# A two-layer hybrid block: x also loaded by columns, first-layer S5 angles on GpSimd, wider kpe and gate products

## The chip, the cores and the metric

The kernel runs on one core of a Trainium2 chip. Its time is that of one execution on the device in microseconds (us); three executions of the kernel before gave 883.68, 882.55 and 882.38, median 882.55. The engines are TensorE (PE in the profile: matrix products and transposes; PEld is its weight load), VectorE (DVE), ScalarE (ACT), GpSimd (POOL) and SyncE (SP), whose queue issues nearly all transfers. Each engine runs its own instructions in a fixed order and waits on semaphores of the others.

## The reference

256 tokens of width 1024 (f32) pass two layers. In each, a normed h is projected once, and three mixers share the columns: latent attention (MLA, 8 heads), a gated linear attention in chunks of 64 (GLA, 4 heads) and a diagonal state-space scan (S5, 32 groups of 64 complex states).

```
h = rms_norm(x, norm1_g[l])
(cq, ckv, kpe, gq, gk, gv, glr, gr, su, gates) = split_in(h @ w_in[l])
o_a = mla_mixer(cq, ckv, kpe, ...)
o_b = gla_mixer(gq, gk, gv, glr, gr, ...)     # log_a = log_sigmoid(g_lr @ w_gate + b_gate) / 16
o_c = s5_mixer(su, ...)                       # lam_bar = exp(lam * step); states by associative scan
g = sigmoid(gates + gate_b[l]).reshape(B, L, 3, D)
merged = g[:,:,0]*(o_a @ w_br_mla[l]) + g[:,:,1]*(o_b @ w_br_gla[l]) + g[:,:,2]*(o_c @ w_br_s5[l])
x = x + merged @ w_out[l]
h2 = rms_norm(x, norm2_g[l])
x = x + square(relu(h2 @ w_ff1[l])) @ w_ff2[l]
```

The kernel does the S5 scan in a rotating frame: it needs, for each of 16 x 128 states, the sine and cosine of angle times position. These depend on the parameters alone.

## The kernel before, in words

**Tiling.** h is kept by columns: 8 tiles of 128 features by 256 tokens, each as a rounded part (hi) and a rest (lo). The weights lie in HBM as 276 chunks of 128x1024 f32 (512 KB). `fetch` (L139) loads a chunk into one of three buffers raw, the first two chunks in halves; `prep` (L155) splits it: ScalarE casts hi (L164), VectorE subtracts to lo (L165). Every product is three: hi by hi, hi by lo, lo by hi (L184 to L186). Chunks are prepared three ahead, in four buffers.

**Start.** `setup` (L264) loads x by token rows in four pieces, with the constants between them, on SyncE's queue. `norm` (L508) turns x by 16 transposes on TensorE (L520), VectorE multiplies by the gain (xs, L523), ScalarE and VectorE split to h. The norm's factor is not put into h: `norm_end` (L529) squares x on ScalarE, VectorE makes the reciprocal root (nr) and two scaled unit matrices dg (L549), and in `norm_rows` TensorE makes from them a row of factors for all partitions, rb (L555), with which later results are multiplied.

**Order of the work.** `mixers` (L1232) walks a hand-written table, STEPS (L1171), one string for each layer. An entry names a step and the offset of its priority: "kg~53" is the next piece of the step kg, 53 further back. The scheduler then places each engine's instructions by priority. qk, kg, gate, gv, gr, core, gout are GLA; ckv, cq, kv, v, kT, q, qT, h, p are attention; su, u, v0 to s3 and y are S5; g and b entries are the gates and the branch products. "P" is the next piece of `s5_pre` (L334), which makes the S5 constants of the first layer between the other steps. The second layer's constants are made during the first layer's feed-forward.

**S5 constants.** `s5_pre` makes roots and exponentials on 128x16 tiles with VectorE, then bbar and cmat (ScalarE spreads z, L418), which TensorE transposes (Btp, L453) and multiplies (K0p, L462). The angles follow (L471 to L499): for each of four tiles ph of 128x512, VectorE multiplies the position iota by the high part of the angle thi, takes off the whole turns (kk, in the buffer cosT), adds iota times the low part (four operations, L485) and takes off the whole turns again. ScalarE makes sine, half-angle sine and its square (L493 to L495), VectorE the cosine from the square (L499). GpSimd does only memsets and the copies R (L606).

**GLA around the change.** `gla_qk` (L903): 96 products of 256 columns to gqkp, rb, then gqk = gqkp times rb. `kpe_glr` (L682): a product kgp of 128 rows, of which rows 0 to 31 are the rotary key and 32 to 47 the gate's low-rank input; kgT = kgp times rb on 48 rows, two transposes of 32 rows (L690). `gla_gate` (L932): four products of 16 rows, gatep (L937), then log sigmoid, a scan cs, its exponentials ep and en, and with them the scores Ap (L977) and the state terms dS.

Of the kernel before, what the change touches and what calls it, by code (L numbers as in the profile page):

```python
# [8 lines left out]
F32 = mybir.dt.float32  # L9
F32R = mybir.dt.float32r  # L10
# [8 lines left out]
DEPTH = 2  # L19
D = 1024  # L20
# [66 lines left out]
class Kern:  # L87
# [51 lines left out]
    def fetch(self, k):  # L139
        l, c = self.stream[k]  # L140
        n = CCOLS.get(c[0], CW)
        raw = self.ring.tile([128, CW], F32, tag="raw", name="raw", bufs=self.NRAW)
        for h in self.halves(k, n):
            self.nc.sync.dma_start(raw[:, h], self.wst[l, CIDX[c], :, h])
        self.raws.append(raw)

    def halves(self, k, n):

        return [slice(0, n // 2), slice(n // 2, n)] if k < self.NHALF else [slice(0, n)]

# [4 lines left out]
    def prep(self, k):  # L155
# [7 lines left out]
        for h in self.halves(k, n):  # L163
            nc.scalar.copy(hi[:, h], raw[:, h])  # L164
            nc.vector.tensor_tensor(out=lo[:, h], in0=raw[:, h], in1=hi[:, h].bitcast(F32), op=ALU.subtract)  # L165
# [86 lines left out]
    def split(self, hi, lo, src, scale=None):  # L252

        nc = self.nc
        if scale is None:
            nc.scalar.copy(hi, src)  # L256
# [7 lines left out]
    def setup(self):  # L264
# [5 lines left out]
        xl = lambda t, n: load(self.x[:, t, n * 512:(n + 1) * 512], self.xin[t * 128:(t + 1) * 128, n * 512:(n + 1) * 512])  # L270
        o = KOFF["iota"][0]
        xl(0, 0)
        load(con[:, 0:o], self.consts[:, 0:o])
        xl(1, 0)
        self.prefetch(1)
        xl(0, 1)
        xl(1, 1)
        self.prefetch(3)
        self.load_par(0)
        load(con[:, o:], self.consts[:, o:KOFF["caus"][0]])  # L280
# [9 lines left out]
        self.sin = k("sin").rearrange("p (t d) -> p t d", t=NT)  # L290

# [42 lines left out]
    def s5_pre(self, l):  # L334
# [135 lines left out]

        phs = [self.s2(f"Q{4 + i}", "ph") for i in range(4)]  # L471
        sinT, cosT = self.b8(1, "sinT"), self.b8(0, "cosT")
        kk = cosT
        for i in range(4):
# [15 lines left out]
        for i in range(4):  # L490
            c = slice(512 * i, 512 * i + 512)
            ph = phs[i]
            nc.scalar.activation(sinT[:, c], ph, AF.Sin, scale=TURN)  # L493
            nc.scalar.activation(ph, ph, AF.Sin, scale=TURN / 2)
            nc.scalar.activation(cosT[:, c], ph, AF.Square)  # L495
# [11 lines left out]
    def norm(self, l, key, n):  # L507
# [17 lines left out]
        if l or key == "n2g":  # L525
            self.norm_end(l, key, n)
# [155 lines left out]
    def kpe_glr(self, l):  # L682
# [4 lines left out]
        nc.vector.tensor_tensor(out=self.kgT[0:48], in0=p[0:48], in1=self.rb[0:48], op=ALU.mult)  # L687
        p = self.pt("kpe", [128, NT, 32])
        for t in range(NT):
            nc.tensor.transpose(p[:, t, :], self.kgT[0:32, t * 128:(t + 1) * 128], self.ident[0:32, 0:32])  # L690
        self.kpe = self.tiny.tile([128, NT, 32], F32, tag="kpe", name="kpe", bufs=1)
        nc.scalar.copy(self.kpe, p)
# [239 lines left out]
    def gla_gate(self, l):  # L932
# [3 lines left out]
        for m in range(2):  # L936
            nc.tensor.matmul(p[:, m, :], lhsT=wg[32:48, m * 128:(m + 1) * 128], rhs=self.kgT[32:48], start=True, stop=True)  # L937
# [211 lines left out]
    def ff2_end(self, l, n, po):  # L1149
# [13 lines left out]
    NHALF = 2  # L1163
# [79 lines left out]
    def run(self):  # L1243
# [138 lines left out]
```

## Time and profile before

| | |
|---|---|
| median of three executions | 882.55 us |
| the profiled execution, its span | 882.19 us, 880.4 us |
| TensorE busy | 861.7 us, 98% |
| VectorE busy | 694.5 us, 79% |
| ScalarE busy | 522.0 us, 59% |
| GpSimd busy | 25.4 us, 3% |
| mean granted TensorE clock | 0.998 |
| read from HBM, over the span | 145.70 MB, 167 GB/s |

The span runs from the first to the last instruction. The first layer's mixers end at about 239 us, when the product wo begins; its feed-forward fills the time to 452; the second layer's mixers run from there to 675, its feed-forward to the end. A row of the timeline gives start and duration; matmuls are pipelined, so the distance from one start to the next, not the duration, is what one costs. In rows of a stretch the count of instructions stands in brackets, and PEclk is the granted share of TensorE's full clock (1.00 is 2.4 GHz).

### The profile page before, as it was taken

Reading aid. Unit: us, or ns where it says so; the run is one execution under the profiler, and the core shown is the slowest. Engines: PE = TensorE matmul, PEld = TensorE weight load, DVE = VectorE, ACT = ScalarE, POOL = GpSimd, SP = SyncE. Lnnn points to the kernel's source line nnn. Section 1 sums busy time; section 2 is a strip of 40 time slices with the busy share of each in tenths; the row PEclk is TensorE's granted clock in tenths of the full one; section 3 lists DMA queues with packets and bytes.
Section 4 is the critical chain, followed back from the end, with each engine's and each line's share of the span. In section 5 each row is a group of like instructions: output and inputs, shape, how many; then the busy total and the mean of one; then the engine's idle time right before and its main releaser. Section 6 shows DMA issues by size and latency. Waiting matters only on the chain.

```text
span 880.4 us, 15290 instructions
## 1 busy us (share of the span) xinstructions
PE 861.7 (98%) x5900; PEld 771.2 (88%) x5900; DVE 694.5 (79%) x1339; ACT 522.0 (59%) x818; POOL 25.4 (3%) x35
## 2 busy tenths in 40 slices
PE   7999999999999999999999999999999999999998
PEld 6889988899988888888888989898999888888886
DVE  7999999987767986996677887899877776666664
ACT  6877887654456575664457647874554654444442
POOL 2000001010000000000000000002000000000000
PEclk9999999999999999999999999999999999999999
DMA  7534434245564565566545544244555555555562
GB/s 265 188 118 143 154 121 145 72 153 177 189 210 153 186 212 168 182 189 203 190 146 168 191 146 150 97 144 135 178 166 170 191 181 192 189 189 188 192 190 92
DMA packets 42264, 147.73 MB, mean 168 GB/s; under 512 B 4688, under 2 KB 5328, under 8 KB 42192
## 3 DMA queue, kind: packets, MB, share of 16 engines
q1 hardware_dynamic: 42192, 146.76, 51.6%
q8 instruction: 46, 0.75, 0.3%
q14 instruction: 26, 0.21, 0.1%
HBM read 145.70 MB, written 1.05 MB: 167 GB/s over the span
## 4 chain that ended last, share of the span: by engine, by line
PE 84%; DVE 10%; ACT 3%; issue 2%; DMA 1%; SPq 0%; DVEq 0%
PE fp L206 14%; PE fp L210 7%; PE fo L184 7%; PE fo L186 7%; PE fo L185 7%; PE gp L184 3%; DVE lo L165 3%; PE gp L185 3%; PE gp L186 3%; PE brp L184 2%; PE brp L186 2%; PE brp L185 2%; PE wo L186 2%; PE wo L184 2%; PE wo L185 2%
## 5 line engine op out<-in xcount | busy, mean ns | idle before, releaser
L165 DVE TENSOR_TENSOR lo<-raw,hi 128x1024 fp32r<-128x1024 f32 (+2 forms) x276 | 333.0, 1208 | 118.6 <-ACT hi L164 117.5
L164 ACT CAST hi<-raw 128x1024 fp32r<-128x1024 f32 (+2 forms) x276 | 286.1, 1038 | 234.0 <-PE fo L186 52.9
L206 PE MATMUL fp<-h,hi 128*128 128x512 f32 x512 | 180.5, 398 | 0.0
L210 PE MATMUL fp<-h,lo 128*128 128x256 f32 x512 | 133.5, 281 | 0.0
L184 PE MATMUL gp<-h,hi 128*128 128x256 f32 x384 | 109.9, 292 | 1.0 <-ACT ppt L875 0.8
L206 PEld LDWEIGHTS fp<-h,hi 128*128 128x128 f32 x512 | 93.9, 188 | 18.1
L186 PE MATMUL gp<-h,lo 128*128 128x256 f32 x384 | 107.8, 286 | 0.0
L185 PE MATMUL gp<-h,hi 128*128 128x256 f32 x384 | 107.4, 285 | 0.0
L210 PEld LDWEIGHTS fp<-h,lo 128*128 128x128 f32 x512 | 96.8, 189 | 5.5
L184 PE MATMUL fo<-hi,r 128*128 128x512 f32 x256 | 100.1, 391 | 0.0
L186 PE MATMUL fo<-hi,r 128*128 128x512 f32 x256 | 99.7, 390 | 0.0
L185 PE MATMUL fo<-lo,r 128*128 128x512 f32 x256 | 99.7, 389 | 0.0
L184 PEld LDWEIGHTS gp<-h,hi 128*128 128x128 f32 x384 | 72.7, 192 | 2.9 <-ACT ppt L875 1.0
L185 PEld LDWEIGHTS gp<-h,hi 128*128 128x128 f32 x384 | 72.6, 191 | 1.0 <-issue 0.5
L186 PEld LDWEIGHTS gp<-h,lo 128*128 128x128 f32 x384 | 72.7, 192 | 0.1
L185 PEld LDWEIGHTS fo<-lo,r 128*128 128x128 f32 x256 | 48.1, 188 | 10.1
L186 PEld LDWEIGHTS fo<-hi,r 128*128 128x128 f32 x256 | 48.1, 188 | 10.2
L184 PEld LDWEIGHTS fo<-hi,r 128*128 128x128 f32 x256 | 48.1, 188 | 8.8
L1133 ACT COPY fa<-fp 128x256 f32<-128x256 f32 x64 | 23.4, 367 | 29.3 <-PE fp L206 29.1
L1134 DVE TENSOR_TENSOR fa<-fa,fp 128x256 f32<-128x256 f32 x64 | 26.2, 416 | 13.7 <-ACT fa L1133 13.7
L1071 ACT ACTIVATE gt<-gt,hgateb 128x256 f32<-128x256 f32 x48 | 21.9, 501 | 9.0 <-DVE gt L1068 8.8
L256 ACT CAST r<-fa 128x512 fp32r<-128x512 f32 x32 | 19.9, 622 | 9.7 <-DVE fa L1135 9.5
(396 smaller groups left out, 1768.0 us busy)
## 6 DMA issues: line engine op xcount, KB each, us to landing
raw<-wst SPq DMA_DIRECT2D x266, 512.0 KB, 3.6
raw<-wst SPq DMA_DIRECT2D x6, 384.0 KB, 3.0
x<-xin SPq DMA_DIRECT2D x4, 256.0 KB, 4.6
raw<-wst SPq DMA_DIRECT2D x4, 256.0 KB, 5.6
bc_raw<-bcin SPq DMA_DIRECT2D x4, 256.0 KB, 3.8
out_dram<-x SPq DMA_DIRECT2D x4, 256.0 KB, 2.0
par<-parin SPq DMA_DIRECT2D x2, 205.0 KB, 5.8
masks<-consts SPq DMA_DIRECT2D x1, 128.0 KB, 3.8
```

The source lines that it names most:

```text
L164: nc.scalar.copy(hi[:, h], raw[:, h])
L165: nc.vector.tensor_tensor(out=lo[:, h], in0=raw[:, h], in1=hi[:, h].bitcast(F32), op=ALU.subtract)
L184: mm(out, lhsT=lt[0], rhs=rt[0], start=start, stop=False)
L185: mm(out, lhsT=lt[0], rhs=rt[1], start=False, stop=False)
L186: mm(out, lhsT=lt[1], rhs=rt[0], start=False, stop=stop)
L206: up = lambda: mm(flat, lhsT=w[0][:, c], rhs=self.h2[:, k].rearrange("p i t -> p (i t)"), start=k == 0, stop=k == KD - 1)
L210: mm(out[:, 0, :], lhsT=w[1][:, c], rhs=self.h[k][0], start=False, stop=False)
L256: nc.scalar.copy(hi, src)
L1071: nc.scalar.activation(g[:, m, :], g[:, m, :], AF.Tanh, scale=0.5, bias=self.small[l]["gateb"][:, c:c + 1])
L1133: nc.scalar.copy(a[:, m], p[:, 1, :])
L1134: self.mark = v.tensor_tensor(out=a[:, m], in0=a[:, m], in1=p[:, 0, :], op=ALU.add)
```

## The change

1. x is passed a second time by columns (`xtin`), loaded into xT by four transfers on ScalarE's queue. `begin_x` splits h straight from it, with the gain as the scale. `norm` isn't called for the first h; `norm_end` is, for the norm's factor, from token rows of x that are now loaded after the first six chunks.
2. The first chunks are loaded and split in pieces, chunk 0 as two quarters and a half, chunks 1 to 3 in halves, in the order of the string BEGIN, into four of the large buffers.
3. The first layer's angles are made by GpSimd. The four operations of L485 become two on the whole tile. ScalarE's sines are kept behind a certain cast in its order.
4. kgT, the kpe transposes and the gate products use all 128 rows.
5. The step qk has two pieces: products, then rb and what it multiplies. Both tables STEPS are new.

```diff
-            nc.scalar.copy(hi, src)
+            self.cast = nc.scalar.copy(hi, src)
             nc.vector.tensor_tensor(out=lo, in0=src, in1=hi.bitcast(F32), op=ALU.subtract)
...
         self.ident = k("ident")
         self.ng = k("ng")
+        i0 = KOFF["ng"][0]
+        load(con[:, i0:o], self.consts[:, i0:o])
+
+        self.begin()
+        for a in self.BEGIN.split():
+            n, i = a[0], int(a[1:])
+            if n == "x":
+                self.begin_x(i)
+            elif n in "wh":
+
+                m = 4 if n == "w" else 2
+                self.begin_w(i // m, (i % m) * CW // m, CW // m)
+            elif n == "t":
+                load(self.x[:, i, :], self.xin[i * 128:(i + 1) * 128, :])
+            elif n == "f":
+                self.prefetch(i)
+            elif n == "p":
+                self.load_par(0)
+                load(con[:, 0:i0], self.consts[:, 0:i0])
+                load(con[:, o:], self.consts[:, o:KOFF["caus"][0]])
...
+    def begin(self):
+        self.new_h()
+        self.nss = self.tiny.tile([128, 2, NT], F32, tag="nss", name="nss", bufs=2)
+        self.xT = self.b8(6, "xT").rearrange("p (k t) -> p k t", k=KD)
+        hl = lambda n: self.ring.tile([128, CW], F32R, tag=n, name=n, bufs=self.NHI)
+
+        self.raws = [self.b8(i, "raw", cols=2048)[:, 0:CW] for i in (0, 1, 4, 8)]
+
+        for k in range(0, KD, 2):
+            self.nc.scalar.dma_start(self.xT[:, k:k + 2, :], self.xtin[:, k * L:(k + 2) * L])
+        for k in range(4):
+            self.prepped[k] = (hl("hi"), hl("lo"))
+
+    def begin_x(self, k):
+
+        nc = self.nc
+        self.split(self.h[k][0], self.h[k][1], self.xT[:, k, :], scale=self.ng[:, k:k + 1])
+
+    def begin_w(self, k, o, n):
+        l, c = self.stream[k]
+        h = slice(o, o + n)
+        self.nc.sync.dma_start(self.raws[k][:, h], self.wst[l, CIDX[c], :, h])
+        self.split(*(y[:, h] for y in self.prepped[k]), self.raws[k][:, h])
...
+        if l == 0:
+            v, tt = nc.gpsimd, nc.gpsimd.tensor_tensor
         phs = [self.s2(f"Q{4 + i}", "ph") for i in range(4)]
...
-            for j in range(4):
-                v.scalar_tensor_tensor(out=ph3[:, j], in0=self.iota, scalar=tlo[:, 4 * i + j:4 * i + j + 1],
-                                       in1=ph3[:, j], op0=ALU.mult, op1=ALU.add)
+            if l:
+                for j in range(4):
+                    v.scalar_tensor_tensor(out=ph3[:, j], in0=self.iota, scalar=tlo[:, 4 * i + j:4 * i + j + 1],
+                                           in1=ph3[:, j], op0=ALU.mult, op1=ALU.add)
+            else:
+                tt(out=kk[:, c].rearrange("p (s c) -> p s c", s=4), in0=self.iota.unsqueeze(1).to_broadcast(b3),
+                   in1=tlo[:, 4 * i:4 * i + 4].unsqueeze(2).to_broadcast(b3), op=ALU.mult)
+                tt(out=ph, in0=ph, in1=kk[:, c], op=ALU.add)
...
+        with self.tc.issue_after(self.cast.ins):
+            for i in range(4):
...
-        nc.vector.tensor_tensor(out=self.kgT[0:48], in0=p[0:48], in1=self.rb[0:48], op=ALU.mult)
-        p = self.pt("kpe", [128, NT, 32])
+        nc.vector.tensor_tensor(out=self.kgT, in0=p, in1=self.rb, op=ALU.mult)
+        p = self.pt("kpe", [128, NT, 128])
         for t in range(NT):
-            nc.tensor.transpose(p[:, t, :], self.kgT[0:32, t * 128:(t + 1) * 128], self.ident[0:32, 0:32])
+            nc.tensor.transpose(p[:, t, :], self.kgT[:, t * 128:(t + 1) * 128], self.ident)
...
-            nc.tensor.matmul(p[:, m, :], lhsT=wg[32:48, m * 128:(m + 1) * 128], rhs=self.kgT[32:48], start=True, stop=True)
+            nc.tensor.matmul(p[:, m, :], lhsT=wg[:, m * 128:(m + 1) * 128], rhs=self.kgT, start=True, stop=True)
...
+    BEGIN = "x0 w0 x1 x2 w1 x3 h2 h4 h6 x4 x5 h1 x6 x7 h3 p0 h5 h7 f5 f6 t0 t1 f7"
...
-        "qk P~-60 kg P~68 P~-15 gv~42 gate~30 P P~-2 P~15 gv su0 P P~-30 su0~-30 gv gv core~-8 ckv core~-98 P "
+        "qk gv~8 gv~-120 P~-45 gv~120 qk~75 P~-52 kg~60 P~68 gv P~22 P~-60 ckv gate core P~-68 P~112 P~-45 su0 "
...
-        for n in range(2):
-            self.norm(0, "n1g", n)
-            self.prepare(n + 1)
         for n in range(2):
             self.norm_end(0, "n1g", n)
```

What the tables and the scheduler make of it is seen in the engines' orders. A row is an instruction with its tiles and, in brackets, the semaphores it waits for.

Before, TensorE ends the first group of products (gqkp) and goes straight to rb, then to the products of the first gv chunk:

```order
L184 MATMUL gqkp<-h,hi 128x256
L185 MATMUL gqkp<-h,hi 128x256
L186 MATMUL gqkp<-h,lo 128x256
L555 MATMUL rb<-dg,ones 128x128 [waits DVE_49,PE_49,Pool_49]
L555 MATMUL rb<-dg,ones 128x128 [waits DVE_49]
L184 MATMUL gvp<-hi,h 128x512 [waits Activation_49]
L185 MATMUL gvp<-lo,h 128x512 [waits DVE_49]
```

Now the same place, the end of the second gv chunk:

```order
L177 MATMUL gvp<-hi,h 128x512
L178 MATMUL gvp<-lo,h 128x512
L179 MATMUL gvp<-hi,h 128x512
L589 MATMUL rb<-dg,ones 128x128 [waits DVE_49,Pool_49]
L589 MATMUL rb<-dg,ones 128x128 [waits DVE_49]
L177 MATMUL gvp<-hi,h 128x512 [waits Activation_49]
L178 MATMUL gvp<-lo,h 128x512
```

24 products gvp, of 512 columns each, have come between gqkp and rb.

Before, around the first transposes of bbar, Btp, TensorE's order is (cp is a product of the attention's projections):

```order
L185 MATMUL gvp<-lo,h 128x512
L186 MATMUL gvp<-hi,h 128x512
L453 MATMUL Btp<-con,bbar 128x128 [waits PE_49,Activation_49,Pool_49]
L453 MATMUL Btp<-con,bbar 128x128 x7
L184 MATMUL gvp<-hi,h 128x512
L185 MATMUL gvp<-lo,h 128x512
L186 MATMUL gvp<-hi,h 128x512
L184 MATMUL cp<-h,hi 128x256
```

Now Btp stands behind the GLA scores Ap, among products of the gr chunk:

```order
L179 MATMUL cp<-h,lo 128x256
L1013 MATMUL Ap<-ep,en 128x128 [waits DVE_49]
L1013 MATMUL Ap<-ep,en 128x128 x7
L177 MATMUL cp<-h,hi 128x256
L178 MATMUL cp<-h,hi 128x256
L179 MATMUL cp<-h,lo 128x256
L177 MATMUL grp<-hi,h 128x512 [waits Activation_49]
L178 MATMUL grp<-lo,h 128x512
L480 MATMUL Btp<-con,bbar 128x128 [waits DVE_49,Pool_49]
L480 MATMUL Btp<-con,bbar 128x128 x3
L179 MATMUL grp<-hi,h 128x512
```

Products sup, cp and grp, and Ap, which followed Btp before, stand ahead of it now.

On GpSimd, ahead of the first copy R, stand now the angles of the first two tiles ph, and the same again for the other two (before, the copy followed the memset of cmask):

```order
L976 MEMSET cmask 128x8 [waits Pool_49]
L508 ISA
L508 TENSOR_TENSOR ph<-con,thi 128x512 [waits DMAHW6_49,DVE_49]
L508 TENSOR_TENSOR ph<-con,thi 128x512
L510 TENSOR_SCALAR cosT<-ph 128x512 [waits DMAHW2_49,DMAHW4_49,Activation_49,Pool_49]
L510 TENSOR_SCALAR cosT<-ph 128x512 [waits Pool_49]
L511 TENSOR_TENSOR ph<-ph,cosT 128x512 [waits Pool_49] x2
L518 TENSOR_TENSOR cosT<-con,s5tlo 128x512 [waits DVE_49,Pool_49]
L518 TENSOR_TENSOR cosT<-con,s5tlo 128x512 [waits Pool_49]
L520 TENSOR_TENSOR ph<-ph,cosT 128x512 [waits Pool_49] x2
L521 TENSOR_SCALAR cosT<-ph 128x512 [waits Pool_49] x2
L522 TENSOR_TENSOR ph<-ph,cosT 128x512 [waits Pool_49] x2
```

Each waits for GpSimd's own one before it; the first for VectorE's thi. "x2" is one for each of two tiles.

ScalarE takes the sines of these tiles between casts of weight chunks:

```order
L249 CAST hi<-raw 128x1024 [waits DMAHW3_49]
L249 CAST hi<-raw 128x1024 [waits DMAHW4_49,PE_49]
L528 ACT_TABLE_LOAD
L528 ACTIVATE sinT<-ph 128x512 [waits Pool_49] x2
L529 ACTIVATE ph<-ph 128x512 [waits Activation_49] x2
L252 ACTIVATE ob<-goT,houtg 128x512 [waits PE_49]
L530 ACTIVATE cosT<-ph 128x512 [waits Activation_49] x2
L528 ACTIVATE sinT<-ph 128x512 [waits Pool_49] x2
...
L249 CAST hi<-raw 128x768 [waits DMAHW5_49,PE_49]
```

The sines wait for GpSimd (Pool) where they waited for VectorE, and the casts behind them wait in the order.

## Rows read from the trace of the kernel before

**Rows 1.** Page, part 1: engines' busy us, share of the span, instructions

```profile
PE 861.7 (98%) x5900; PEld 771.2 (88%) x5900; DVE 694.5 (79%) x1339; ACT 522.0 (59%) x818; POOL 25.4 (3%) x35
```

**Rows 2.** Stretches: length, busy us of each engine, PEclk, DMA share, GB/s

```profile
110.00:200.00 90.00, 85.41 (x792) 78.93 (x791) 85.35 (x177) 61.74 (x120) 8.63 (x8) 1.00 0.39 122
...
500.00:640.00 140.00, 137.79 (x1206) 130.81 (x1205) 123.27 (x258) 89.32 (x160) 6.77 (x6) 1.00 0.44 141
```

**Rows 3.** Timeline of TensorE, first layer: start, duration, instruction [idle before]

```profile
8.00 0.58 PE L184 MATMUL gqkp<-h,hi 128*128 128x256 f32 x1 [1.43 <-ACT h L256]
...
12.79 0.28 PE L185 MATMUL gqkp<-h,hi 128*128 128x256 f32 x1
12.91 0.28 PE L186 MATMUL gqkp<-h,lo 128*128 128x256 f32 x1
...
22.74 0.61 PE L555 MATMUL rb<-dg,ones 128*128 128x128 f32 x4
...
238.55 0.40 PE L184 MATMUL wo<-hi,mh 128*128 128x512 f32 x1
```

**Rows 4.** Timeline of all engines, the first 6 us

```profile
0.73 1.28 ACT L533 ACT_TABLE_LOAD   x1 [0.73 <-PEq L1375]
...
0.73 0.38 SPq L269 DMA_DIRECT2D x<-xin  x1
...
3.28 0.63 ACT L533 ACTIVATE junk<-x 128x512 bf16<-128x512 f32 x1 [1.27 <-DMA x<-xin]
```

**Rows 5.** Busy time in the first 17 us, GB/s at the end

```profile
0.00:17.00 17.00, 11.16 (x65) 10.12 (x66) 10.96 (x40) 10.93 (x20) 6.09 (x14) 1.00 0.76 254
```

**Rows 6.** Timeline of VectorE, from the sum of squares to dg

```profile
13.62 0.15 DVE L537 TENSOR_TENSOR nms<-nss 128x2 f32<-128x2 f32 x1
...
20.16 0.48 DVE L549 TENSOR_SCALAR dg<-con,nr_y 128x128 f32<-128x128 f32 x2
```

**Rows 7.** Timeline of TensorE at the stall

```profile
43.38 0.39 PE L186 MATMUL gvp<-hi,h 128*128 128x512 f32 x1
45.93 1.17 PE L453 MATMUL Btp<-con,bbar 128*128 128x128 f32 x8 [2.16 <-issue]
```

**Rows 8.** The stretch behind the stall, columns as Rows 2

```profile
48.00:50.20 2.20, 2.20 (x11) 2.10 (x11) 1.96 (x3) 2.14 (x6) 0.00 (x0) 0.51 0.00 0
```

**Rows 9.** Tile ph, 50 to 100 us: count, ns min/median/max, first to last start

```profile
L485 DVE SCALAR_TENSOR_TENSOR ph<-con,s5tlo,ph x16: 343/346/348, 58.0 to 98.6; 128x128 f32<-128x128 f32 x16
L479 DVE TENSOR_TENSOR ph<-con,thi x4: 679/686/689, 55.6 to 73.1; 128x512 f32<-128x512 f32 x4
L481 DVE TENSOR_SCALAR cosT<-ph x4: 417/420/421, 56.6 to 75.9; 128x512 f32<-128x512 f32 x4
```

**Rows 10.** Timeline of GpSimd: three copies of one shape

```profile
148.18 3.92 POOL L606 COPY R<-s5r 128x512 f32<-128x512 f32 x1 [20.85 <-DVE arec L877]
...
163.03 0.61 POOL L606 COPY R<-s5r 128x512 f32<-128x512 f32 x1 [10.76 <-DVE rot L620]
...
304.61 0.64 POOL L606 COPY R<-s5r 128x512 f32<-128x512 f32 x1 [92.98 <-DVE s5lbr L374]
```

**Rows 11.** Timeline of VectorE beside two of these copies

```profile
148.02 0.67 DVE L624 TENSOR_TENSOR rot<-rot,cosT 128x512 f32<-128x512 f32 x1
148.61 0.69 DVE L625 TENSOR_TENSOR rot<-rot,sinT 128x512 f32<-128x512 f32 x1
...
151.55 0.69 DVE L1068 TENSOR_TENSOR gt<-gp,rb 128x512 f32<-128x512 f32 x1
...
304.68 0.59 DVE L383 TENSOR_TENSOR s5t<-s5lbi,par 128x16 f32<-128x16 f32 x1
305.19 0.16 DVE L386 TENSOR_TENSOR s5pi<-s5lbi,s5re 128x16 f32<-128x16 f32 x1
```

**Rows 12.** Timeline of TensorE, second layer: rb and the first wo product

```profile
464.28 0.61 PE L555 MATMUL rb<-dg,ones 128*128 128x128 f32 x4
...
675.42 0.40 PE L184 MATMUL wo<-hi,mh 128*128 128x512 f32 x1
```

More of the change, by code (lines that the diff above doesn't have):

```diff
@@ L142, in fetch @@
         raw = self.ring.tile([128, CW], F32, tag="raw", name="raw", bufs=self.NRAW)
-        for h in self.halves(k, n):
-            self.nc.sync.dma_start(raw[:, h], self.wst[l, CIDX[c], :, h])
+        self.nc.sync.dma_start(raw[:, 0:n], self.wst[l, CIDX[c], :, 0:n])
         self.raws.append(raw)
-    def halves(self, k, n):
-        return [slice(0, n // 2), slice(n // 2, n)] if k < self.NHALF else [slice(0, n)]
     def prefetch(self, n):
@@ L162, in prep @@
         lo = self.ring.tile([128, CW], F32R, tag="lo", name="lo", bufs=self.NHI)
-        for h in self.halves(k, n):
-            nc.scalar.copy(hi[:, h], raw[:, h])
-            nc.vector.tensor_tensor(out=lo[:, h], in0=raw[:, h], in1=hi[:, h].bitcast(F32), op=ALU.subtract)
+        self.split(hi[:, 0:n], lo[:, 0:n], raw[:, 0:n])
         return hi, lo
@@ L269, in setup @@
         load = lambda dst, src: nc.sync.dma_start(dst, src)
-        xl = lambda t, n: load(self.x[:, t, n * 512:(n + 1) * 512], self.xin[t * 128:(t + 1) * 128, n * 512:(n + 1) * 512])
         o = KOFF["iota"][0]
[L272 to L280, printed above, removed]
         k = lambda n: con[:, KOFF[n][0]:KOFF[n][0] + KOFF[n][1]]
@@ L489, in s5_pre @@
             yield
[L490 to L495, printed above, removed]
+        with self.tc.issue_after(self.cast.ins):
+            for i in range(4):
+                c = slice(512 * i, 512 * i + 512)
+                ph = phs[i]
+                nc.scalar.activation(sinT[:, c], ph, AF.Sin, scale=TURN)
+                nc.scalar.activation(ph, ph, AF.Sin, scale=TURN / 2)
+                nc.scalar.activation(cosT[:, c], ph, AF.Square)
         yield
@@ L524, in norm @@
             self.split(*(y[:, n * 4:n * 4 + 4, t * 128:(t + 1) * 128] for y in self.hs), xs)
-        if l or key == "n2g":
-            self.norm_end(l, key, n)
+        self.norm_end(l, key, n)
     def norm_end(self, l, key, n):
@@ L686, in kpe_glr @@
         self.kgT = self.rp("kgT")
-        nc.vector.tensor_tensor(out=self.kgT[0:48], in0=p[0:48], in1=self.rb[0:48], op=ALU.mult)
-        p = self.pt("kpe", [128, NT, 32])
+        nc.vector.tensor_tensor(out=self.kgT, in0=p, in1=self.rb, op=ALU.mult)
+        p = self.pt("kpe", [128, NT, 128])
         for t in range(NT):
-            nc.tensor.transpose(p[:, t, :], self.kgT[0:32, t * 128:(t + 1) * 128], self.ident[0:32, 0:32])
+            nc.tensor.transpose(p[:, t, :], self.kgT[:, t * 128:(t + 1) * 128], self.ident)
         self.kpe = self.tiny.tile([128, NT, 32], F32, tag="kpe", name="kpe", bufs=1)
-        nc.scalar.copy(self.kpe, p)
+        nc.scalar.copy(self.kpe, p[:, :, 0:32])
     def att_c(self, l, nm):
@@ L906, in gla_qk @@
         self.ws4(P, [self.w(l, ("gq", i)) for i in range(2)] + [self.w(l, ("gk", i)) for i in range(2)])
+        yield
         self.norm_rows()
@@ L1161, in ff2_end @@
             self.norm(l + 1, "n1g", n)
-    NHALF = 2
+    BEGIN = "x0 w0 x1 x2 w1 x3 h2 h4 h6 x4 x5 h1 x6 x7 h3 p0 h5 h7 f5 f6 t0 t1 f7"
     NPS = {"g": 2, "ps": 2, "acc": 4}
@@ L1191, in table @@
         T = {
-            "qk": ([r("gq", 2) + r("gk", 2)], self.gla_qk), "kg": (e("kg", 1), self.kpe_glr), "gate": ([[]], self.gla_gate),
+            "qk": ([r("gq", 2) + r("gk", 2), []], self.gla_qk), "kg": (e("kg", 1), self.kpe_glr), "gate": ([[]], self.gla_gate),
             "gv": (e("gv", 4), self.gla_vr, "gv"), "gr": (e("gr", 4), self.gla_vr, "gr"), "core": ([[]] * 3, self.gla_core),
@@ L1358, in pack_inputs @@
     return {
-        "xin": a["x"].reshape(L, D), "wst": wst, "parin": par, "bcin": bc.reshape(DEPTH, 128, 1024),
+        "xin": a["x"].reshape(L, D), "xtin": a["x"].reshape(L, KD, 128).transpose(2, 1, 0).reshape(128, KD * L),
+        "wst": wst, "parin": par, "bcin": bc.reshape(DEPTH, 128, 1024),
         "consts": con,
```

25 rows, old and new, of the table STEPS are left out of this document.

## The prediction

> **What bounds the kernel now.** The page's first part comes first: TensorE is busy 98% of an 880.4 us span, VectorE 79% [rows 1]. So only time that TensorE stands still, or runs slow, can be won; the number of matmuls hardly changes. The table by stages then shows where that is: the feed-forward stages are full, while from 110 to 200 us TensorE has 85.41 us of 90 busy, with VectorE at 85.35; the same part of the second layer, 500 to 640, misses 2.2 of 140 [rows 2]. The timeline of TensorE from the start shows the other two losses. The first product begins at 8.00 and the 96 of that group end at 22.74, when rb begins; at full speed they are 0.12 us apart [rows 3], so 96 take 11.4 us and the rest is start. And at 43.38 the last product before a stall begins, its successor Btp at 45.93 [rows 7]; behind the stall 11 matmuls, the first and the last cut by the edges, fill 2.20 us at a granted clock of 0.51, the lower level (1.2 GHz) [rows 8]. What Btp waits for is ScalarE's copies of bbar, which wait for VectorE, so in this stretch VectorE sets the end.
>
> **Start of the kernel.** The 16 transposes, the products with the gain and the splits of h go; ScalarE makes h from columns of x. It now issues four transfers first. An issue takes 0.38 on SyncE, and the table load, 1.28, stands behind them instead of at 0.73 [rows 4]; the fourth also waits until the first has landed. A 256 KB piece issued at 0.73 is followed by ScalarE's first use at about 3.3 in the trace; with smaller first pieces I put the landing at 2.9. 2.9 + 1.28 = 4.2; a scaled copy of 256 columns and a cast of a quarter, together about the 0.63 of one operation on 512 columns [rows 4], and a semaphore: first matmul at 5.0. Before, products that begin at 8.00 have their full spacing only by 12.79 [rows 3]; I keep 4.3 us of such a beginning, at the 0.21 a product of the slow stretch behind the stall [rows 8]. That is 20 products, which at 0.12 would take 2.4: 1.9 extra. 5.0 + 11.4 + 1.9 = 18.3 for the end of the group, against 22.74: **-4.4** (between -6 and -2, for later landings).
>
> Behind it rb now comes later in TensorE's order, after 24 products of 512 columns, some 5.4 us: TensorE is there at 23.7. rb needs the row norms, and these need x by rows, which is loaded behind 4.4 MB: x by columns (1), six weight chunks (3) and the tables (0.4). Before, 4.3 MB had arrived by 17 us (254 GB/s) [rows 5]; two more 512 KB pieces at that rate land by 21. Four squares of 0.63 on ScalarE begin with the first piece, so the sums are complete at about 21. From the sum to the first dg took 6.54 us before (13.62 to 20.16), among other work [rows 6]; with less in between 5 to 6. So rb is ready at about 26: a wait of 2 to 3, with the lower clock behind it perhaps 4, at best 0.5 if the chain is packed closer. **+2.5**.
>
> **The stall at 43 us.** Btp and K0p are later in the new table: Ap and the score products of GLA go ahead, and TensorE reaches Btp about 12 us of its own work later, which VectorE has to use. The 2.3 us of standing and some 2.0 us of slow clock behind it [rows 7, 8] go: -4.3. What is late next is en, on VectorE, for which Ap waits: adding the durations in the new orders up to there, VectorE has 3.2 us more work than TensorE, as against up to 17 us in the old order; with the start as above 0.4 us of wait remains, before anything GpSimd does.
>
> **The angles on GpSimd.** VectorE loses 16 operations of 0.346, 12 like the 0.686 row, and 12 like the 0.420 row, the 4 final scalings among them [rows 9]: 18.8 us as recorded. Starts lie closer than that, 0.59 apart for 0.67 [rows 11], so 15.4 in the order. GpSimd gets 20 two-input products and 12 scalings of 128x512. The trace has none of these on GpSimd. The nearest rows are its copies of that size, one input: 0.61 alone [rows 10]. Two inputs read one after the other would be 1.22, which I take; 0.61 is the lower end, and the 3.92 of a delayed copy the upper end. By the Trainium skill, GPSIMD Engine Reference, section 3.1, a two-input addition is 1.96 times as slow there as on VectorE; with VectorE's 0.686 that estimates 1.34, and 20 of them 2.4 us more than by my value.
>
> More important is what they do to VectorE. The copy at 148.18 lasts 3.92 because VectorE runs one two-input operation after another; it ends when an operation begins at 151.55 that reads PSUM [rows 10, 11]. In the other direction, while the copy at 304.61 (0.64) ran, a tiny VectorE product lasted 0.59 in place of 0.16 [rows 10, 11]. So each GpSimd operation slips in at an operation that leaves room, and then holds the next two-input one. Held time per GpSimd operation: 0 at least, 0.43 in the trace for a copy of 0.64, up to 1.0 for 1.22. Ten of the 28 stand ahead of en in time. At 0.4 each this is 4.0 us at Ap (0 to 6.3): the stall becomes -4.3 + 0.4 + 4.0 = **+0.1** (bounds -3.9 and, with the low clock again, +4.4). Over all 28 it is 11 us, of 15.4 freed.
>
> **110 to 200 us.** VectorE enters this stretch with 4 us less behind it, and TensorE's missing 4.6 us and the close waits around it (the chain there runs through VectorE's lo products) can shrink. But the second layer, without angles or Btp, needs from rb to the first wo product 675.42 - 464.28 = 211.1 us, and the first layer 238.55 - 22.74 = 215.8 [rows 3, 12], of which 4.3 are the stall above and about 2.4 Btp and K0p, which the second layer does elsewhere. So the first layer is already no worse than one with a free VectorE, and I take only **-3** (between -9, if VectorE's whole relief arrives, and +2).
>
> The kpe transposes and gate products on all rows are 6 instructions of the same columns on TensorE; they hide behind streaming weights: 0, at most 0.3 either way. The second layer's new table moves work in stages where TensorE is full: 0, give or take 1.
>
> Sum: -4.4 + 2.5 + 0.1 - 3 = -4.8, from the profiled 882.19 (0.4 below the median of 882.55): **877 us**.
>
> **Rivals.** *GpSimd holds VectorE longer than it relieves it.* 20 x 1.22 + 8 x 0.61 = 29 us of GpSimd time in a stretch in which VectorE is never idle. From 15.4 / 28 = 0.55 us lost for each operation the move costs more than it frees, and the row of 0.59 for a GpSimd operation half as long speaks for that; the many short operations that read PSUM, beside which GpSimd costs nothing, against. Then: start -4.4, rb +4, Ap -4.3 + 6.7 + 2 of slow clock, +2 after 110: +6, **888 us**. The Trainium skill, SBUF — State Buffer, section Who interferes with whom, says that whichever of the two begins holds the shared ports for its whole instruction and the other fully blocks; by that rule this rival is the full price, and the two rows above agree with it.
>
> *Only the start is won.* The waits between 110 and 200 are latencies of attention and scan, which the second layer pays too, and the freed VectorE only waits longer: -4.4 + 2.5 + 0.1 + 0 = -1.8, **880.4 us**. The comparison of the layers speaks for it, VectorE's 95% for less.
>
> *The relief arrives whole.* The first dg comes early (+0.5), GpSimd takes only room that VectorE leaves (-3.9 at the stall), -9 after 110: -16.9, **865 us**. For it: VectorE is the close limit in the old order until 100 us. Against it: the 0.43 above.
>
> *GpSimd is late.* ScalarE's sines now wait for GpSimd and stand ahead of casts; if the 28 are not done when ScalarE gets there, some 82 to 97 us, casts and then matmuls wait. With 2 us for each, wait and work, it ends by 25 + 28 x 2 = 81, just in time; the copy of 3.92 shows that one can take twice that. Some 6 us late it costs -1.8 + 4 (two of the six covered by casts made ahead) + 1 of clock: **885 us**.
>
> **How the numbers follow.** Forecast 0.40, its own range 873 to 880; GpSimd holds 0.20; start only 0.20; whole relief 0.15; late GpSimd 0.05. Within 0.2% (1.8 us) a measurement of this kernel can't be told from no change. Faster: nearly all of the forecast, the whole relief and half of the start-only case, 0.63. Same: the other part of that and margins, 0.12. Slower: 0.25. The range reaches from the whole relief to just short of the first rival: 864 to 887.
>
> **What would show it.** First matmul at 5.0 and the first group ended by 18.3; rb waiting for dg at about 24 to 26; no stall at Btp, but one of some 4 us at Ap for VectorE's en; two-input operations on GpSimd of about 1.2 us, VectorE's short products stretched to 0.6 and more beside them; sines on ScalarE that start without waiting. The forecast is wrong if Ap doesn't wait at all, if TensorE still stands as long from 110 to 200, or if VectorE between 25 and 90 us does its other work later than before.

## The result: 2.5% slower

The changed kernel takes 905.28 us (median of 4, 903.16 to 906.81) against 882.46 (median of 4, 882.32 to 883.68): ratio 1.0254, 95% interval 1.0229 to 1.0279, 22.8 us more. The forecast was 877 in a range of 864 to 887. Of its rivals the first, that GpSimd holds VectorE longer than it relieves it, has the mechanism of more than half of the loss; its 888 was too low as well.

The page's first part of the changed kernel, answering to [rows 1]:

```profile
PE 866.7 (96%) x5884; PEld 773.7 (85%) x5884; DVE 706.0 (78%) x1302; ACT 518.0 (57%) x823; POOL 73.3 (8%) x67
```

GpSimd's busy time rises from 25.4 to 73.3 us. VectorE, which was to lose some 15 us, is busy 11.5 us longer, in 37 instructions fewer. The stretches show where TensorE loses the time (length, busy us and count of PE, PEld, DVE, ACT and POOL, PEclk, DMA share, GB/s; the last one answers to the first of [rows 2]):

```profile
20.00:43.00 23.00, 14.32 (x68) 11.48 (x66) 21.14 (x70) 13.01 (x24) 14.95 (x11) 0.93 0.49 173
43.00:62.00 19.00, 15.80 (x95) 13.96 (x95) 19.00 (x29) 9.65 (x19) 19.00 (x12) 0.91 0.27 84
62.00:110.00 48.00, 40.47 (x346) 35.76 (x347) 37.79 (x79) 29.21 (x47) 14.39 (x9) 0.93 0.40 124
110.00:200.00 90.00, 85.40 (x687) 80.36 (x685) 84.51 (x195) 69.36 (x135) 5.71 (x10) 0.98 0.38 118
```

The first three before:

```profile
20.00:43.00 23.00, 23.00 (x150) 20.32 (x149) 21.32 (x86) 18.40 (x26) 0.72 (x2) 1.00 0.60 187
43.00:62.00 19.00, 16.84 (x187) 14.30 (x185) 17.13 (x36) 14.18 (x28) 0.00 (x0) 0.91 0.30 105
62.00:110.00 48.00, 47.97 (x346) 44.56 (x346) 45.03 (x138) 37.16 (x58) 0.00 (x0) 1.00 0.48 156
```

From 20 to 62 us VectorE is busy nearly throughout, GpSimd from 28 on, and TensorE has 30.12 us of 42 (14.32 + 15.80); before, it had 39.84. From 62 to 110, where it was full before (47.97 of 48), it misses 7.5 us. From 110 to 200 it is busy as long as before. The timeline of TensorE has the marks of [rows 3] and what took the place of [rows 7] (start, duration, instruction, idle before it):

```profile
6.69 0.58 PE L177 MATMUL gqkp<-h,hi 128*128 128x256 f32 x1 [6.69 <-ACT hi L249]
...
19.91 0.39 PE L177 MATMUL gvp<-hi,h 128*128 128x512 f32 x1
...
25.86 0.40 PE L179 MATMUL gvp<-hi,h 128*128 128x512 f32 x1
31.21 1.19 PE L589 MATMUL rb<-dg,ones 128*128 128x128 f32 x4 [4.96 <-DVE dg L583]
...
77.49 0.72 PE L1013 MATMUL Ap<-ep,en 64*128 64x128 f32 x8 [3.75 <-DVE en L999]
```

The first matmul comes at 6.69 (forecast 5.0; before, the first product at 8.00), the group of 96 ends at 19.9 (forecast 18.3, before 22.74). rb then waits 5 us instead of 2 to 3, and Ap begins at 77.49; in the kernel before Ap's products lay between 50.9 and 53.3. All long waits of TensorE in between are for VectorE:

```profile
PE rb L589 <- DVE dg L583: 5.0, 1, 5.0
PE cp L177 <- DVE gqk L946: 4.2, 1, 4.2
PE Ap L1013 <- DVE en L999: 3.7, 1, 3.7
PE cp L179 <- DVE lo L250: 2.2, 1, 2.2
PE cp L177 <- DVE ckv L253: 2.2, 1, 2.2
```

A measure for what follows, worked out from the timelines: for each matmul, its distance to the next start less the usual distance of that shape (the 30th percentile in the kernel before), summed by stretch. It is called lost time below; the 16 transposes that the new start removes are 1.7 us besides.

| kernel | first matmul | to 24 us | 24 to 100 | of it to 60 | 100 to 160 | 160 to 240 | 240 to 480 | from 480 |
|---|---|---|---|---|---|---|---|---|
| before | 3.58 | 6.0 | 9.7 | 7.6 | 13.8 | 10.6 | 3.2 | 24.1 |
| changed | 6.69 | 2.5 | 30.0 | 16.0 | 11.0 | 17.1 | 3.8 | 26.6 |
| changed, angles on VectorE | 6.65 | 2.6 | 11.1 | 5.7 | 17.2 | 11.5 | 3.9 | 25.4 |
| changed, no angles | 6.82 | 2.3 | 11.4 | 7.5 | 16.3 | 9.9 | 3.8 | 25.3 |
| before, only the start | 6.72 | 3.4 | 16.9 | 13.3 | 12.7 | 12.1 | 4.2 | 24.8 |
| ... and no first squares | 6.55 | 4.3 | 12.3 | 8.8 | 13.6 | 16.2 | 4.2 | 26.7 |
| before, only angles on GpSimd | 3.63 | 6.2 | 21.5 | 11.3 | 10.2 | 13.9 | 3.0 | 24.7 |
| before, only tables, kpe and gate | 3.70 | 5.5 | 14.9 | 5.1 | 14.7 | 16.8 | 3.2 | 25.4 |

In the kernels with the old start the first matmul is a transpose. Each row is one execution: that without squares was the slowest of its four (893.33, median 890.66), that with the angles on VectorE the fastest of its five (887.39, median 890.88). Most of the loss, 20.3 us more than before, lies between 24 and 100 us; from 160 to 240 it is 6.5 more, and the rest nearly cancels out.

GpSimd runs its 28 angle operations back to back through that time (an x2 row is two of them):

```profile
28.05 2.06 POOL L508 TENSOR_TENSOR ph<-con,thi 128x512 f32<-128x512 f32 x2 [21.43 <-DVE nr_t L223]
30.08 4.13 POOL L510 TENSOR_SCALAR cosT<-ph 128x512 f32<-128x512 f32 x2
...
70.98 4.29 POOL L522 TENSOR_TENSOR ph<-ph,cosT 128x512 f32<-128x512 f32 x2
75.22 1.07 POOL L640 COPY R<-s5r 128x512 f32<-128x512 f32 x1
```

From 28.05 to 75.22 it never pauses: 1.68 us for each operation. And VectorE, beside it (the rows answer to those of [rows 11]):

```profile
28.11 1.00 DVE L224 SCALAR_TENSOR_TENSOR nr_t<-nr_t,nms 128x2 f32<-128x2 f32 x1
29.04 0.16 DVE L239 SCALAR_TENSOR_TENSOR s5er<-s5er,expr 128x16 f32<-128x16 f32 x1
29.12 1.01 DVE L391 SCALAR_TENSOR_TENSOR s5tlo<-thi,s5tlo 128x16 f32<-128x16 f32 x1
30.06 0.15 DVE L225 SCALAR_TENSOR_TENSOR nr_y<-nr_t,nr_y 128x2 f32<-128x2 f32 x1
...
46.33 1.21 DVE L250 TENSOR_TENSOR lo<-raw,hi 128x1024 fp32r<-128x1024 f32 x1
47.47 1.52 DVE L433 TENSOR_TENSOR z<-z,s5lbr 128x256 f32<-128x256 f32 x1
48.91 1.51 DVE L436 TENSOR_TENSOR z<-bc_raw,s5pr 128x256 f32<-128x256 f32 x1
```

Short operations of 0.16 last 1.00, products z of 0.42 last 1.52; in the chain of short ones every second keeps its usual length. Taking from each VectorE operation between 28 and 76.5 us the median of its like elsewhere, 28 of 69 are stretched, by some 21 us in all, 0.75 each: nearly one for each of GpSimd's 28 and the copy R behind them. In the kernel before none is.

### The profile page after: what moved, and what is told of

It is laid out like the page before. It is cut to its first block, busy times and chain, and to the rows that moved or that the text cites. A ratio compares the mean times of both kernels' runs of the same rounds, so it can differ in the third digit from the quotient of the medians.

```text
span 905.0 us, 15273 instructions
## 1 busy us (share of the span) xinstructions
PE 866.7 (96%) x5884; PEld 773.7 (85%) x5884; DVE 706.0 (78%) x1302; ACT 518.0 (57%) x823; POOL 73.3 (8%) x67
## 4 chain that ended last, share of the span: by engine, by line
PE 80%; DVE 10%; ACT 5%; DMA 3%; issue 2%; SPq 0%; DVEq 0%; ACTq 0%
PE fp L199 13%; PE fp L203 7%; PE fo L177 6%; PE fo L178 6%; PE fo L179 6%; PE gp L177 4%; PE gp L178 4%; PE gp L179 4%; PE brp L177 2%; PE brp L179 2%; PE brp L178 2%; DVE lo L250 2%; PE wo L178 2%; PE wo L177 2%; PE wo L179 2%
## 5 line engine op out<-in xcount | busy, mean ns | idle before, releaser
L250 DVE TENSOR_TENSOR lo<-raw,hi 128x1024 fp32r<-128x1024 f32 (+3 forms) x279 | 337.7, 1212 | 119.1 <-ACT hi L249 117.6
L249 ACT CAST hi<-raw 128x1024 fp32r<-128x1024 f32 (+3 forms) x279 | 286.0, 1029 | 220.3 <-PE fo L179 48.6
L178 PEld LDWEIGHTS fo<-lo,r 128*128 128x128 f32 x256 | 48.1, 188 | 10.2
L640 POOL COPY R<-s5r 128x512 f32<-128x512 f32 x8 | 12.1, 1508 | 301.4 <-DVE rot L654 210.1
L177 PE MATMUL cp<-h,hi 128*128 128x256 f32 x80 | 23.7, 299 | 7.7 <-DVE gqk L946 4.2
```

The lines of the kernel that those rows point to most:

```text
L177: mm(out, lhsT=lt[0], rhs=rt[0], start=start, stop=False)
L178: mm(out, lhsT=lt[0], rhs=rt[1], start=False, stop=False)
L249: self.cast = nc.scalar.copy(hi, src)
L250: nc.vector.tensor_tensor(out=lo, in0=src, in1=hi.bitcast(F32), op=ALU.subtract)
L640: nc.gpsimd.tensor_copy(R3, s["r2"][:, r].unsqueeze(2).to_broadcast([128, 4, 128]))
```

## Experiments

Each time stands with its ratio to the kernel before, timed beside it (medians of 882.5 to 883.5), and the ratio's 95% interval. Two theories: (A) GpSimd's operations hold VectorE where VectorE sets the end; (B) the late row norms and the new tables cost the time.

**One part undone, one part alone.** The changed kernel with the angles on VectorE:

```diff
-        if l == 0:
-            v, tt = nc.gpsimd, nc.gpsimd.tensor_tensor
...
-            if l:
+            if True:
                 for j in range(4):
```

> The changed kernel with the first layer's angles back on VectorE (four scalar_tensor_tensor for each tile, as before); start, wide kpe and gate products and both tables stay as changed. Theory A (GpSimd's 28 operations hold VectorE's two-input operations, 21 us between 28 and 76 us, where VectorE sets the end): 905 falls to 878 to 888, VectorE's operations there have their usual lengths, Ap begins near 55 instead of 77. Theory B (the late row norms behind the new start, and the new tables, are what costs): 898 or more.

890.88 us, ratio 1.0097 (1.0071 to 1.0122). 14.4 us of the 22.8 are GpSimd's (15.4 when each kernel is taken against the kernel before timed beside it); between 28 and 76.5 us hardly a VectorE operation is stretched, and Ap begins at 56.8. The rest, over 7 us, is more than A expected. Only the angles moved, in the kernel before (the lines of the diff on the angles, with `issue_after`):

> The kernel before with only the first layer's angles moved to GpSimd; start, kpe and gate products and tables as before. Theory A: slower by 10 to 22 us (892 to 905), with some 28 VectorE operations stretched by about 0.75 us each between 25 and 75 us. Theory B: 880 to 885, since GpSimd has time enough and VectorE 15 us less to do.

894.54 us, 1.0130 (1.0108 to 1.0152), with 20 operations stretched by some 14 us in all, as A says. Only the new start (the changed setup, with the old tables, angles, kpe and gate products; ScalarE's sines stay behind the cast):

> The kernel before with only the new start (x by columns, first chunks in pieces, token rows late); angles on VectorE, kpe and gate products and both tables as before, so that rb stands right behind the 96 products. Theory A: the 96 products end near 20 instead of 22.7, but rb then waits for the row norms until about 29: 884 to 890, no gain. Theory B: 890 or more. If the start is worth what was forecast (-4.4 +2.5): 880.

890.35 us, 1.0083 (1.0060 to 1.0107). The start doesn't gain, it costs 7 us, though rb comes at 26.94, behind products gvp, and isn't waited for. Both old tables in the changed kernel:

> The changed kernel with both old tables and qk in one piece; new start, angles on GpSimd, wide kpe and gate products stay. Theory A: GpSimd still holds VectorE for about 21 us, 898 to 912. Theory B, if the new tables are what costs: 880 to 888.

902.79 us, 1.0221 (1.0196 to 1.0245): with GpSimd's operations in it the kernel is slow with either pair of tables, as A says. Yet alone, in the kernel before, the new ones are bad:

> The kernel before with only the new tables, qk in two pieces and the kpe and gate products on all rows; start and angles as before. If the parts add up (start 7, angles on GpSimd 12 to 14, whole change 22.8): 882 to 886.

895.22 us, 1.0143 (1.0128 to 1.0158). So the parts don't add up: 7 (start), 11 (angles) and 12.5 (tables, kpe and gate products) alone, 7.4 for start and tables together, 19 for start, angles and the wide products, 22.8 for all. The new tables cost next to nothing with the new start (7.4 against 7) and 12.5 without it.

**What holds VectorE.** In the kernel before nothing is moved, and GpSimd gets 28 operations that nobody needs, released by thi:

```diff
         kk = cosT
+        if l == 0:
+            ga = phs[3]
+            nc.gpsimd.tensor_copy(ga[:, 0:16], thi)
+            for i in range(28):
+                nc.gpsimd.tensor_copy(ga.rearrange("p (s c) -> p s c", s=4), self.iota.unsqueeze(1).to_broadcast([128, 4, 128]))
```

> The kernel before, with nothing moved, and 28 extra copies of 128x512 on GpSimd (they read SBUF and write a tile that VectorE first needs for its third angle), released by thi as the angles were. If it is GpSimd's reading of SBUF that holds VectorE: some 25 VectorE operations are stretched, by 0.4 to 0.6 each, between 28 and 65 us, and the time rises by 5 to 13 us (888 to 896). If it was only the moved work or what waits for it: 882 to 885.

890.92 us, 1.0091 (1.0074 to 1.0108). Then `nc.gpsimd.memset(ga, 0.0)` in place of the copy:

> As the copies, but 28 memsets of the same size, which write SBUF and read nothing. If only reading holds VectorE: no VectorE operation is stretched, 882 to 885. If any work on GpSimd does: as the copies, 888 to 896.

882.55 us, 0.9997 (0.9987 to 1.0006). The groups of GpSimd's operations (count, busy, mean ns) and a group of VectorE's z (ns min/median/max), first with the copies:

```profile
L476 POOL COPY ph<-con 128x512 f32<-128x512 f32 x28 | 24.5, 874 | 1.6
```

```profile
L408 DVE TENSOR_TENSOR z<-z,z x3: 823/824/825, 47.6 to 54.3; 128x256 f32<-128x256 f32 x3
```

And with the memsets:

```profile
L476 POOL MEMSET ph<- 128x512 f32 x28 | 14.7, 526 | 1.5
```

```profile
L408 DVE TENSOR_TENSOR z<-z,z x3: 422/424/426, 41.6 to 44.6; 128x256 f32<-128x256 f32 x3
```

Beside copies z lasts 0.824, beside memsets 0.424, its usual time. With the copies 27 VectorE operations are stretched, by some 10 us in all. It is the reading of SBUF on GpSimd that keeps VectorE out; writing doesn't. The Trainium skill, SBUF — State Buffer, section Who interferes with whom, states just this for VectorE operations with two SBUF inputs; the two rows of z agree. Seven copies of 128x2048 move the same bytes:

> The kernel before with 7 extra GpSimd copies of 128x2048 in place of the 28 of 128x512 (890.9, 27 VectorE operations stretched by 10.1 us in all): the same bytes. If VectorE loses by the operation, 7 operations are stretched by some 0.4 each, 3 us, and the time is 882 to 885. If it loses by GpSimd's time, because whoever holds keeps the other out to its end: 6 or 7 operations are stretched by 1.5 to 2.3 us each, 10 to 15 us in all, and the time is 889 to 896.

894.61 us, 1.0132 (1.0115 to 1.0149), 7 operations stretched by some 11 us in all: VectorE loses by GpSimd's time, not by the number of operations. The timelines of GpSimd (one copy) and of VectorE in that run show how they take turns:

```profile
41.97 2.13 POOL L477 COPY cosT<-con 128x2048 f32<-128x2048 f32 x1
```

```profile
41.85 0.16 DVE L383 TENSOR_TENSOR s5t<-s5lbi,par 128x16 f32<-128x16 f32 x1
41.93 0.42 DVE L409 TENSOR_TENSOR z<-bc_raw,s5lbr 128x256 f32<-128x256 f32 x1
42.27 1.86 DVE L384 TENSOR_TENSOR s5pr<-s5pr,s5t 128x16 f32<-128x16 f32 x1
44.05 0.16 DVE L386 TENSOR_TENSOR s5pi<-s5lbi,s5re 128x16 f32<-128x16 f32 x1
44.13 1.21 DVE L165 TENSOR_TENSOR lo<-raw,hi 128x1024 fp32r<-128x1024 f32 x1
45.27 1.86 DVE L385 TENSOR_TENSOR s5pr<-s5pr,s5den 128x16 f32<-128x16 f32 x1
```

VectorE gets two operations, a short one and one of 0.4 or 1.2, then the next lasts until the copy is done: the copy ends at 44.10, s5pr at 44.13, after 1.86 in place of 0.16.

**Where the hold falls.** The second layer's angles on GpSimd instead (`if l == 1`), made in the first layer's feed-forward:

> The kernel before with the second layer's angles on GpSimd (they are made during the first layer's feed-forward, where VectorE has about a quarter of its time free and TensorE is full); the first layer's stay on VectorE. If the cost comes from where the hold falls: VectorE is stretched by a similar sum, 10 to 20 us, and the time stays within 1.5 us of before (882 to 885). If the operations cost wherever they stand: 892 or more.

900.12 us, 1.0197 (1.0182 to 1.0212). This kernel also kept the first layer's sines behind a cast, which the kernel before doesn't. Without that (the second layer's sines stay behind one):

> As the run with the second layer's angles on GpSimd (900.1), with the first layer's sines as in the kernel before. Its trace showed 21 us of stretched VectorE operations and 12 us of TensorE waits between 300 and 360 us, and 5 more waits between 140 and 200, where only the first layer's sines differ: 893 to 896. If those 5 came from GpSimd: 899 to 901.

893.37 us, 1.0118 (1.0102 to 1.0134). So the operations cost 10 us even where VectorE has a fifth of its time free and TensorE was full. The stretch from 300 to 360 us, before and then with these angles on GpSimd:

```profile
300.00:360.00 60.00, 60.00 (x371) 51.05 (x370) 48.48 (x103) 38.94 (x63) 0.74 (x2) 1.00 0.57 185
```

```profile
300.00:360.00 60.00, 51.69 (x315) 43.01 (x314) 59.16 (x83) 32.13 (x53) 51.13 (x30) 0.94 0.47 149
```

VectorE, in 20 instructions fewer, goes from 48.48 to 59.16: some 21 us of stretching are added where 12 were free, and TensorE loses 8.3. My first expectation, no cost, was wrong.

The other runs with free sines, as in the kernel before (`if True:` in place of the `with` line):

> As the run with only the new start (890.4), but ScalarE's sines are no longer kept behind a cast. In the trace of that run some of the added waits lie between 100 and 200 us, where only the sines differ from before. If keeping them back costs: 885 to 888. If the start alone costs the 7 us: 889.5 to 892.

> As the changed kernel with the angles back on VectorE (890.9), but ScalarE's sines are not kept behind a cast. If keeping them back costs: 884 to 888. If not: 889.5 to 892.

> As the run with only the angles on GpSimd (894.5), sines not kept behind a cast. GpSimd's hold stays (14 us of stretched VectorE operations in that run), so 889 to 895; if keeping the sines back made the 11 us, 882 to 885.

896.52 (ratio 1.0152, 1.0110 to 1.0194), 891.85 (1.0100, 1.0081 to 1.0120) and 903.61 us (1.0232, 1.0175 to 1.0290). The first and the third came out above every value that I had for them. Keeping the sines back is no cost of the change: where the first layer's angles move or the start does, it helps or makes no difference. Where neither does, it cost about 7 us (900.12 against 893.37); why is not shown.

**What the relief is worth.** The angles left out altogether:

> The kernel before, leaving out the 36 VectorE operations of the first layer's angles (four GpSimd memsets, which hold nothing, set the tiles instead). This is the most that moving them could be worth. If the angles stand where TensorE is full anyway (55 to 100 us): 878 to 883. If VectorE's 15 us are worth what the whole-relief rival said: 868 to 874.

> The changed kernel, leaving out the first layer's angles in the same way (the four scalings of the cosine on VectorE). Against the changed kernel with the angles on VectorE (890.9) this is what the relief is worth in the new order; against the changed kernel (905) the whole price of having them on GpSimd. If the relief is worth little: 886 to 891; if much: 875 to 882.

886.53 (1.0041, 1.0022 to 1.0060) and 887.72 us (1.0050, 1.0034 to 1.0066). In the kernel before, 36 VectorE operations less make it 4 us slower: the scheduler moves other work into their places, and by 100 us TensorE has lost 4.7 us more than before. In the changed kernel they are worth about 3 us (890.88 less 887.72). So the price of the angles on GpSimd is 17.6 us (905.3 less 887.7), and what it could have bought is 3. The stretch of the hold, in the changed kernel, with the angles on VectorE, and without them:

```profile
28.00:76.50 48.50, 32.15 (x187) 28.66 (x187) 48.26 (x71) 27.44 (x44) 48.35 (x30) 0.89 0.35 114
```

```profile
28.00:76.50 48.50, 46.26 (x396) 40.78 (x394) 45.34 (x111) 34.46 (x59) 0.72 (x2) 1.00 0.46 147
```

```profile
28.00:76.50 48.50, 45.43 (x399) 41.07 (x399) 39.37 (x93) 35.55 (x62) 0.72 (x2) 1.00 0.46 141
```

With the angles on VectorE, TensorE is busy 46.26 of 48.5 us, as good as without them (45.43): in this stretch VectorE's 6 us more cost nothing.

**What the start costs.** Rows of x two chunks earlier (`h3 t0 t1 p0 h5 h7 f5 f6 f7`), in the changed kernel with the angles on VectorE:

> The changed kernel with the angles back on VectorE (890.9 in the first experiment) and x by token rows loaded two 512 KB chunks earlier, ahead of the tables and the rest of chunk 2 and 3. If rb's wait for the row norms is what the start costs: row sums 2 to 3 us earlier, 886 to 889. If the start costs because the first 23 us now carry 1 MB more: weights come later instead, 889 to 893.

890.44 us, 1.0090 (1.0075 to 1.0105) against 890.88: no difference. Without the first squares, then with the rows loaded later as well:

> The kernel before with only the new start (890.4), leaving out the first norm's squares on ScalarE (its sums are a constant set by GpSimd at the start, so the row norms wait for no token rows; the rows are still loaded as early). If the squares and the late norm behind them, now in a stretch where casts are due, make the start's 7 us: 883 to 887. If the megabyte of rows in the first 23 us does: 889 to 891.

> As the kernel without the first norm's squares, and the token rows are loaded some 10 us later, behind the first GLA steps (left out: the same squares). What it gains over that kernel is the traffic's share: 0 to 1 us if the work made the cost, 3 to 6 us if traffic did. Together 878 to 884.

890.66 (1.0093, 1.0074 to 1.0113) and 885.80 us (1.0035, 1.0020 to 1.0050). In the sum, then, the squares cost nothing and the rows 5 us. The lost time says more: without squares TensorE loses 12.3 instead of 16.9 us from 24 to 100, and gives it back from 160 to 240 (16.2 for 12.1); with the later rows it is 11.3, and 8.9 there. ScalarE's timeline of the start alone shows squares where casts are due:

```profile
18.17 0.63 ACT L565 ACTIVATE junk<-x 128x512 bf16<-128x512 f32 x1 [1.53 <-DMA x<-xin]
...
21.24 0.63 ACT L565 ACTIVATE junk<-x 128x512 bf16<-128x512 f32 x1
...
26.28 1.28 ACT L395 ACT_TABLE_LOAD   x1
...
29.00 1.04 ACT L249 CAST hi<-raw 128x1024 fp32r<-128x1024 f32 x1
```

and TensorE's waits from 20 to 60 us:

```profile
PE Btp L480 <- ACT Bt L481: 2.2, 1, 2.2
PE gvp L177 <- ACT hi L249: 2.0, 1, 2.0
PE Btp L480 <- issue: 1.9, 1, 1.9
```

The two middle squares lie between the first two rows, with a cast; before, all four were done by 13.1 us, about when the first group reached its full spacing [rows 3]. The table load stands at 25.81 in the kernel before as well. The last row is the cast for which gvp waits 2.0 us; without squares that wait is gone. So up to 100 us the squares and what waits for them cost some 4.6 us, but leaving them out gains nothing in the end, and the rows' 5 us lie mostly behind 100. What sets the waits from 160 to 240, which change by up to 7 us between kernels with the same work there, is not settled, and so the start's 7 us are explained only in part. Angles on ScalarE were not tried. No run beats the kernel before.

**Where the gains of start and tables go.** First matmul and lost time together tell how far behind a kernel is at 60 us: 17.2 before, 14.9 in the changed kernel with the angles on VectorE, which also has 1.7 of transposes less to do. So there it is 4.0 us ahead, and no stall at Btp is left. From 60 to 160 it loses 22.6, where the kernel before loses 15.9. The kernel with only the new tables is 2.9 ahead at 60 and loses 24.5 up to 160. In both TensorE waits long for hq_y, a row factor of the attention that VectorE makes; before, it waits 0.3 for it. The changed kernel with the angles on VectorE, then only the tables:

```profile
PE gp L177 <- DVE hq_y L225: 3.6, 1, 3.6
```

```profile
PE gp L184 <- DVE hq_y L232: 3.7, 1, 3.7
```

Where nothing is moved to GpSimd, the kernels with the new first-layer table lose more from 60 to 160 (20.2 without the angles, to 24.5) than those with the old one (15.9, to 19.1 with the start and free sines). Which entry of the table does it was not tried.

## Why the prediction was wrong

Forecast (-4.8) and result (+22.8) lie 27.6 us apart, in two parts. The angles on GpSimd cost 15.4 over the changed kernel with the angles on VectorE; the forecast had +4.0 at Ap and -3 after 110, 14.4 less. The changed kernel with the angles on VectorE costs 7.4; the forecast had -4.4 + 2.5 for the start and -4.3 + 0.4 for the stall, 13.2 less.

- **The hold of an operation.** The first step that failed is "At 0.4 each this is 4.0 us at Ap", "Over all 28 it is 11 us, of 15.4 freed". Measured: 0.75 each, some 21 over all. The 0.4 was the row of a copy of 0.64 [rows 11], applied to operations put at up to twice that; with that row's own proportion (0.43 held of 0.64) an operation of 1.0 would have given 0.7. The price of 1.22 for two inputs was near: the first two lasted 2.06 together, and VectorE's operations beside them 1.00 each in place of 0.16.
- **Ten of the 28 ahead of en.** All 28 were: the hold makes VectorE's chain to en longer, GpSimd goes on meanwhile, and Ap begins 2.2 us after the last one ends. The wait at Ap alone was 3.75 (forecast 4.4), but gqk, ckv, lo and u, all on VectorE, were waited for on the way.
- **What lets GpSimd in.** I took it that it needs an operation that leaves room, as the one at 151.55 that reads PSUM [rows 11]. In the chain of small dependent operations it gets in at about every second one. The 3.92 of the delayed copy [rows 10] was the case of long operations back to back.
- **The relief.** 15.4 us fewer for VectorE were credited in full against the hold. They lay at 55 to 101 us [rows 9], where TensorE was full nearly throughout, and are worth about 3 us. The -3 after 110 didn't come: between 100 and 160 us TensorE loses 2.8 less than before, but between 160 and 240 6.5 more.
- **The start and the stall.** The second step that failed is that what they win by 60 us lasts to the end; the sum takes it so without a reason. With the angles on VectorE 4.0 of the forecast 5.8 were there at 60 us: the first group ends 2.8 earlier, rb comes at 26.33 without a wait, Btp isn't waited for, and Ap for 1.3. Then more than that was lost again, with the new table; the cause in the table stays open. The first group came 1.6 later than forecast since ScalarE's table load begins at 4.54, behind four issues that took 3.78, and not at 2.9:

```profile
0.73 3.78 ACTq L304 DMA_DIRECT2D xT<-xtin  x4
...
4.54 1.28 ACT L252 ACT_TABLE_LOAD   x1 [4.54 <-DMA xT<-xtin]
```

- **The wait for rb.** In the changed kernel it was 5 us: the sums were there at 23.5 (21.3 with the angles on VectorE), the mask for which a cast ahead of the norm waits at 24.2, and GpSimd's first operations stretched the norm's chain and its neighbours by 2.1 us.
- **Tables.** "0, give or take 1" for the second layer's was nearly right (from its first product to its first feed-forward product 247.8 us, before 246.4). The prediction gives the first layer's table only gains; alone, with kpe and gate products, the tables cost 12.5.
- **Rival one** had the mechanism and the condition (0.55 lost an operation; it was 0.75) but a price of 6, of which the start's and the stall's gains were part.
- **A slip.** The whole relief adds up to -16.8, not -16.9; nothing hangs on it.

## What to carry to other kernels

Before work is moved to GpSimd, ask what VectorE runs beside it: here a GpSimd operation that reads SBUF kept a VectorE operation out until it was done, and 28 of them cost VectorE some 21 us, more than the 15.4 it was relieved of; fewer and longer operations were no help, memsets were free. And ask where the relief falls: VectorE's time freed where TensorE was full was worth about 3 us in one order, and in the other cost 4, because everything else moved. A gain early on is not yet a gain at the end: 4 us won by 60 us were lost by 160.

## What was not expected of the hardware

- Both engines advance in turns, with no long wait for either: 28 operations took 47.2 us, 1.04 the shortest of two inputs and 0.62 a scaling alone, and VectorE's stretched ones 0.75 us longer each.
- One-input VectorE operations are held too: the subtraction of a constant on 128x16 (s5nr, 0.22 before) lasted 1.24 at 39.78 us, and beside a copy of 128x2048 a scaling of 128x16 (s5tlo) 1.91.
- Products that read PSUM were not held: gqk, four times, 0.41 on average, and kgT 0.41, in the middle of it.
